# The loop over further expert blocks moved between the 24th and the 25th expert, the last block's results in float32, sums of squares as products with ones

## The chip, the cores and the metric

One core of a Trainium2 chip runs the whole program. The metric is the device time of one execution in microseconds (us); the median of the runs counts. Five engines work side by side, each through its own list of instructions: PE multiplies matrices, DVE and ACT work on vectors, POOL on vectors and scattered transfers, and SP issues the transfers of the weights. They wait for each other, and for transfers, by semaphores.

## The reference

Two layers. Each is a mixer (state space, attention, long convolution; the change only touches what it receives) and then a mixture of 32 experts, of which every token uses two. At the end comes a normalisation.

```python
def _rms_norm(x, g):
    xf = x.astype(jnp.float32)
    y = xf * lax.rsqrt(jnp.mean(xf * xf, axis=-1, keepdims=True) + EPS)
    return (y * g.astype(jnp.float32)).astype(x.dtype)

def _hier_moe(h, w_group, w_expert, w1, w3, w2):
    ...
    g_w, g_idx = lax.top_k(g_prob, 1)
    top_v, top_i = lax.top_k(in_group, MOE_TOP_K)
    gate = jax.nn.softmax(top_v, axis=-1) * g_w
    ...
    def expert_block(args):
        xb, e = args
        return (jax.nn.silu(xb @ w1[e]) * (xb @ w3[e])) @ w2[e]
    ...
    ys = ys.reshape(n_rows, d) * row_w[:, None].astype(h.dtype)
    return jnp.zeros_like(h).at[row_tok].add(ys)

def reference(x, c, ctx, ...):
    for i in range(DEPTH):
        hl = _modulate(xl, norm1_g[i], mod_l[0], mod_l[1])
        ...
        xl = xl + mod_l[5] * y          # y: the experts' sum for each token
    return _rms_norm(xl, final_g)
```

Width 1024, 256 latent tokens and 256 context tokens; the experts' hidden width is 512. Layer 0 treats all 512 tokens, layer 1 the 256 latent ones.

## The kernel before, in words

The residual stream xT lies transposed in the chip's memory: 128 partitions times 8 pieces (k) of the width, with the tokens as columns (512 in layer 0, 256 in layer 1).

Each expert has one block of 64 places for tokens. Its weights are 12 pages of 512 KB: 8 pages w13 (w1 beside w3) and 4 pages w2. SP issues their loads in the order of use, through 8 semaphores that it takes in turn, so each load waits for the one 8 before it: 8 loads are in flight. `Stream.pump` holds how many pages SP may be ahead of PE: 18 in layer 0 from the 17th expert on, 30 in layer 1. All pages come from one pool of 44.

For each expert PE runs `first_half` (w13: 16 products, L1582), waits for ACT and DVE (`swiglu`, then `turn`), and runs `second_half` (w2: 8 products, L1606). Then `scaled_result` takes the 64x1024 results times the token's weight as a rounded high part and the remainder: ACT, DVE, ACT, DVE, one after the other (L118, L1718). Two experts share a tile of 128 rows; `combine` brings the pair before back to its tokens by two products per k with a 0/1 matrix GT (L1688), and `residual` adds them to xT on DVE (L1620). Those products fill the gaps of the next experts.

Layer 0 always runs a 33rd block for the first expert with more than 64 tokens. Whatever is still left over goes through a loop whose count is read from the data (`tc.For_i`, L1900). With this data the count is 0 in both layers: no row of the trace comes from the loop's body. The loop stands at the end of each layer's experts.

`combine_last` brings the last block back (layer 1: the last pair), spreads k over more banks of PSUM and interleaves squares of xT (ACT) and their sum (DVE); for k = 0, 2, 4 the addition runs on ACT and POOL. After the loop the sum of squares goes through `rstd_columns` (products with ones into columns of 1, square root, reciprocal of 128x4 or 128x2) and is spread back over rows by transposes (L217). Layer 0 hands this to the first projections of layer 1; layer 1 to the final stage (L1956, then the output's transfers).

Experts are counted from 0 here: e = 24 is the 25th.

Of the kernel before, what the change touches and what calls it, by code (L numbers as in the profile page):

```python
# [69 lines left out]
def build(tc, A, dbg=None):  # L70
# [1333 lines left out]
    def moe(i, pctx, router, ws, last_part):  # L1404
# [380 lines left out]
        def extra_result(b, inf1):  # L1785

            Y_[-1] = [page(F32R) for _ in range(2)]
            scaled_result(Y_[-1], b, inf1[:, 1:2], slice(0, CAP))
            GT_[-1] = wk([128, n], "GT", 2, F32R)
            nc.vector.tensor_scalar(GT_[-1][0:CAP], iotaN[0:CAP, 0:n], inf1[0:CAP, 0:1], None, op0=OP.is_equal)  # L1790
# [286 lines left out]
```

## Time and profile before

| | us |
|---|---|
| runs | 1707.82, 1708.36, 1708.34 |
| median | 1708.34 |
| profiled execution, its own time | 1709.9 |
| its span | 1708.1 |
| PE busy | 1533.8 |
| DVE busy | 888.6 |
| ACT busy | 482.4 |

The span is the time from the first to the last instruction; 1.8 us of the execution's own time lie around it. PE is busy for 90% of the span, but that is a mean over stages, so the places that the change touches are read by themselves: e = 24 of layer 0 begins at 796.12 us, the hand-off of layer 0 at 944.29 us (the end of the 33rd block's w2 products), e = 24 and e = 31 of layer 1 begin at 1564.07 and 1671.08 us, and layer 1's w2 products end at 1686.56 us.

### The profile page before, as it was taken

What the parts mean: (1) busy time and instruction counts of PE and PEld (TensorE: products, weight loads), DVE (VectorE), ACT (ScalarE), POOL (GpSimd) and SP (SyncE); (2) the same over time, 40 slices, a digit from 0 to 9 for tenths busy, and PEclk for the clock granted to TensorE, in tenths of its full rate; (3) what the DMA queues carried; (4) which work ended last, traced back from release to release, by engine and by line L of the source; (5) the groups of instructions that cost most, each with busy time, mean ns of one, the idle gap of its engine ahead of it and who ended that gap; (6) DMA issues with size and microseconds to landing.
All of it is one profiled execution on the core that took longest, in us unless ns stands there. A gap on an engine that the chain in (4) does not pass through costs nothing. (4 is left out here: it accounts for less than half of the span.)

```text
span 1708.1 us, 22533 instructions
## 1 busy us (share of the span) xinstructions
PE 1533.8 (90%) x8073; PEld 788.0 (46%) x8073; DVE 888.6 (52%) x2176; ACT 482.4 (28%) x931; POOL 94.7 (6%) x154
## 2 busy tenths in 40 slices
PE   5888889998999999999899597899799999999995
PEld 1676744476433333344233387547534444333322
DVE  6769565545244546864643758455524434333333
ACT  3343544342111121112122534444311111111112
POOL 0000212003000000002000000010100000000000
PEclk9998899998999999999999698998899999999998
DMA  9111244559999999999999112577799999999994
GB/s 343 64 38 62 79 181 162 218 198 351 374 392 407 409 409 409 409 408 372 373 402 409 61 62 99 205 264 267 293 359 409 409 409 409 409 409 409 409 409 184
DMA packets 143300, 510.04 MB, mean 299 GB/s; under 512 B 17995, under 2 KB 18573, under 8 KB 142929
## 3 DMA queue, kind: packets, MB, share of 16 engines
q1 hardware_dynamic: 138736, 495.21, 75.0%
q0 software_dynamic: 4160, 12.82, 2.2%
q8 instruction: 66, 1.08, 0.3%
q10 hardware_dynamic: 288, 0.52, 0.1%
q14 instruction: 50, 0.40, 0.1%
HBM read 504.85 MB, written 3.64 MB: 298 GB/s over the span
## 5 line engine op out<-in xcount | busy, mean ns | idle before, releaser
L1582 PE MATMUL MOEp<-MOEpg,MOEpg 128*64 128x512 f32 x956 | 227.4, 603 | 13.1 <-DMA MOEpg<-in_w 11.9
L1582 PE MATMUL MOEp<-MOEpg,ROUTpg 128*64 128x512 f32 x960 | 220.5, 603 | 8.2 <-DMA MOEpg<-in_w 7.9
L1718 DVE SCALAR_TENSOR_TENSOR MOEpg<-MOEpY,MOEwt,MOEpg 64x512 fp32r<-64x512 f32 x128 | 96.0, 750 | 241.5 <-ACT MOEpg L118 241.4
L1606 PE MATMUL MOEpY<-MOEpg,MOEhT 128*64 128x512 f32 x960 | 219.4, 599 | 1.8 <-DVE MOEhT L1598 1.8
L1620 DVE SCALAR_TENSOR_TENSOR zxT<-MOEpC,zmod,zxT 128x256 f32<-128x256 f32 x385 | 168.2, 479 | 8.2 <-PE MOEpC L1698 2.1
L118 ACT ACTIVATE MOEpg<-MOEpY,MOEwt 64x512 fp32r<-64x512 f32 x128 | 87.3, 682 | 276.3 <-PE MOEpY L1606 212.2
L1588 DVE TENSOR_TENSOR MOEh<-MOEh,MOEp 128x256 f32<-128x256 f32 x65 | 27.3, 420 | 241.9 <-ACT MOEh L118 241.9
L118 ACT ACTIVATE MOEh<-MOEp 128x256 f32<-128x256 f32 x65 | 24.9, 383 | 399.7 <-PE MOEp L1582 399.7
L1688 PE MATMUL MOEpC<-MOEGT,MOEpg 128*128 128x512 f32 (+1 forms) x496 | 130.0, 364 | 6.7 <-DVE zxT L1620 6.0
L1582 PEld LDWEIGHTS MOEp<-MOEpg,ROUTpg 128*64 128x64 f32 x960 | 64.2, 137 | 149.4 <-issue 103.7
L1582 PEld LDWEIGHTS MOEp<-MOEpg,MOEpg 128*64 128x64 f32 x956 | 59.4, 136 | 159.3 <-DMA MOEpg<-in_w 90.5
L1606 PEld LDWEIGHTS MOEpY<-MOEpg,MOEhT 128*64 128x64 f32 x960 | 63.5, 136 | 120.6 <-issue 93.8
L1688 PEld LDWEIGHTS MOEpC<-MOEGT,MOEpg 128*128 128x128 f32 x496 | 75.2, 189 | 61.7 <-issue 26.8
L166 PE MATMUL ADAb<-ADApg,zcact 128*32 128x512 f32 x384 | 76.1, 614 | 12.8 <-DMA ADApg<-in_adaw 12.8
L788 PE MATMUL PROJb<-INPpg,PROJpg 128*128 128x512 f32 (+1 forms) x384 | 73.8, 356 | 6.4 <-DVE PROJpg L974 5.7
L788 PEld LDWEIGHTS PROJb<-INPpg,PROJpg 128*128 128x128 f32 x384 | 63.5, 206 | 15.9 <-ACT PROJpg L118 6.7
L118 ACT ACT_TABLE_LOAD x35 | 44.9, 1283 | 15.7 <-DVE ATTst L1102 5.7
L1657 PE MATMUL MOEpG<-MOEpg,ROUTpg 128*128 128x256 f32 x240 | 44.7, 310 | 1.1 <-DVE MOEpg L1493 1.1
L1657 PEld LDWEIGHTS MOEpG<-MOEpg,ROUTpg 128*128 128x128 f32 x240 | 33.0, 194 | 24.2 <-issue 15.8
L1091 PE MATMUL ATTb<-QKVpg,QKVpg 96*128 96x512 f32 x64 | 35.4, 654 | 7.3 <-ACT ATTpg L118 7.3
L1373 PE MATMUL OUTb<-OUTpg,ATTpg 128*128 128x512 f32 (+1 forms) x192 | 41.3, 380 | 0.0
L1373 PEld LDWEIGHTS OUTb<-OUTpg,ATTpg 128*128 128x128 f32 x192 | 34.9, 214 | 5.3 <-DVE ATTpg L230 0.2
(541 smaller groups left out, 2115.2 us busy)
## 6 DMA issues: line engine op xcount, KB each, us to landing
MOEpg<-in_w SPq DMA_DIRECT2D x719, 512.0 KB
ADApg<-in_adaw SPq DMA_DIRECT2D x96, 512.0 KB
ROUTpg<-in_w SPq DMA_DIRECT2D x61, 512.0 KB
PROJpg<-in_win SPq DMA_DIRECT2D x16, 512.0 KB
ATTpg<-in_wout SPq DMA_DIRECT2D x8, 512.0 KB
OUTpg<-in_wout SPq DMA_DIRECT2D x8, 512.0 KB
QKVpg<-in_uq SPq DMA_DIRECT2D x5, 512.0 KB
MOEpg<-in_win SPq DMA_DIRECT2D x5, 512.0 KB
```

What stands on the lines that cost most here:

```text
L118: nc.scalar.activation(out, in_, f, **kw)
L166: nc.tensor.matmul(b[q:q + 32, :], cact[:, k, :], w[:, h * 512:(h + 1) * 512], start=(k < 2), stop=(k >= KD - 2), tile_position=(0, q))
L788: nc.tensor.matmul(b, a_[:, c], b_[k][:, c0:], start=(first and n == 0), stop=(last and n == 2))
L1091: nc.tensor.matmul(b, qc[h][:, nq - NS + qt * 128:nq - NS + (qt + 1) * 128], kc[h], start=True, stop=True)
L1373: nc.tensor.matmul(b, a_[:, c], y_, start=(n == 0 and j == 0), stop=(n == KD - 1 and j == 2))
L1582: nc.tensor.matmul(b[64 * h:64 * h + 64, :], X[:, k, :], w[:, h * 512:(h + 1) * 512], start=(k == 0), stop=(k == KD - 1), tile_position=(0 ...
L1588: nc.vector.tensor_mul(h_, h_, b[:, 256:512])
L1606: nc.tensor.matmul(b[64 * h:64 * h + 64, :], hT[:, k % 2, (k // 2) * 64:(k // 2) * 64 + 64], w[:, h * 512:(h + 1) * 512], start=(k == 0), ...
L1620: nc.vector.scalar_tensor_tensor(xT[:, k, seg(s)], b[:, s * NS - c0:(s + 1) * NS - c0], mod[:, 40 + k, s:s + 1], xT[:, k, seg(s)], op0=OP. ...
L1657: nc.tensor.matmul(b[:, kk * 256:(kk + 1) * 256], hs[t][:, k * 128:(k + 1) * 128], G[:, t].rearrange("p e c -> p (e c)"), start=(t == 0 an ...
L1688: nc.tensor.matmul(b, Y_[p][j][rows, k * 128:(k + 1) * 128], GT_[p][rows], start=(j == 0), stop=(j == 1))
L1718: nc.vector.scalar_tensor_tensor(Y[1][rows_of, h * 512:(h + 1) * 512], b[rows], wt[rows], yh.bitcast(F32), op0=OP.mult, op1=OP.subtract)
```

## The change

```diff
+FURTHER = 24
+    def rstd_rows(b, r, nch):
+        act(r, b, AF.Sqrt, scale=1.0 / nch, bias=epsT)
+        nc.vector.reciprocal(r, r)
+        return r
...
-            rstd1 = rstd_of(None, D, acc=acc)
-            first_projections(rstd1)
+            first_projections(acc)
...
+        def combine_last(y, gt):
+            total = pb("pT")[:, 0:n]
+            for k in range(KD + 3):
+                if k < KD:
+                    b = pb(*tags[k % 5])[:, 0:n]
+                    nc.tensor.matmul(b, y[:, k * 128:(k + 1) * 128], gt, start=True, stop=True)
+                    if i == 0 and k in (0, 3):
...
+                    else:
+                        residual(b, k)
+                if 1 < k < KD + 2:
+                    sq[k - 2] = squares()[:, 0:n]
+                    act(sq[k - 2], xT[:, k - 2, c0:], AF.Square)
+                if k > 2:
+                    nc.tensor.matmul(total, ones2[:, 0:1].to_broadcast([128, 128]), sq.pop(k - 3),
+                                     start=(k == 3), stop=(k == KD + 2))
+            return rstd_rows(total, squares()[:, 0:n], D)
...
+        def places(idx, wt, rows):
+            nc.vector.tensor_scalar(gt, iotaN[rows, 0:n], idx, wt, op0=OP.is_equal, op1=OP.mult)
+        def plain_result(b, rows):
+            y = page()[rows]
+            for h in range(2):
+                copy(h, y[:, h * 512:(h + 1) * 512], b[64 * h:64 * h + 64])
...
+        def last_hook(k):
+            last = NE // 2 - 1
+            if k < 4:
+                combine(last - 1, [4 + k])
+            else:
+                combine(last, [2 * k - 8, 2 * k - 7], slice(0, CAP))
...
-            for e in range(NE):
+            for e in range(FURTHER):
+                expert(e)
+        further_blocks()
+        with tc.manual_schedule():
+            for e in range(FURTHER, NE):
+                expert(e)
...
-        nc.vector.memset(item, 0.0 if i == 0 else -1.0)
-        with tc.For_i(0, nc.values_load(items, min_val=0, max_val=2 * NT // CAP), 1):
```

In words: (1) the loop stands between e = 23 and e = 24 in both layers; its body, which does not run, uses 2 pages as a ring and adds straight into xT. (2) The last block (layer 0: the 33rd; layer 1: e = 31) keeps its results plain, half copied by ACT and half by DVE; the token's weight is in GT; one float32 product per k takes the place of two. In layer 1, e = 30 is brought back inside `first_half` of e = 31, by `last_hook`, with the four products left of the pair before. (3) The squares are summed by float32 products with ones in all 128 rows, so the sum stands in every partition; square root and reciprocal then run over 128x512 (layer 0) or 128x256 (layer 1), and `rstd_columns` and the transposes go. (4) POOL adds for k = 0 and 3 in layer 0 only; the final gain is loaded early.

The next pieces are the programs' orders, one row per instruction, with what it waits for; DMAHW0 to 7 are the eight semaphores of SP's loads, DMASW those of POOL's, and the "_49" says nothing here. First SP, before, at the loop of layer 1: the branches follow the last loads of expert weights (the last page of e = 31).

```order
L114 DMA MOEpg_12371<-in_w 128x1024 [waits DMAHW5_49,PE_49]
L114 DMA MOEpg_12375<-in_w 128x1024 [waits DMAHW6_49,PE_49]
L114 DMA MOEpg_12379<-in_w 128x1024 [waits DMAHW7_49,PE_49]
L114 DMA MOEpg_12383<-in_w 128x1024 [waits DMAHW0_49,PE_49]
L114 DMA MOEpg_12387<-in_w 128x1024 [waits DMAHW1_49,PE_49]
L114 DMA MOEpg_12391<-in_w 128x1024 [waits DMAHW2_49,PE_49]
L1900 COMPARE_AND_BRANCH
L1900 UNCONDITIONAL_BRANCH [waits SP_sequencer_49,DMAHW0_49,DMAHW1_49,DMAHW2_49,DMAHW3_49,DMAHW4_49,DMAHW5_49,DMAHW6_49,DMAHW7_49]
```

SP now, at the same loop: the row ahead of the branch is the load of page 317 (counted from 1), that is of the 5th page of e = 26.

```order
L115 DMA MOEpg_11758<-in_w 128x1024 [waits DMAHW4_49,PE_49]
L115 DMA MOEpg_11792<-in_w 128x1024 [waits DMAHW5_49,PE_49]
L115 DMA MOEpg_11796<-in_w 128x1024 [waits DMAHW6_49,PE_49]
L115 DMA MOEpg_11800<-in_w 128x1024 [waits DMAHW7_49,PE_49]
L115 DMA MOEpg_11804<-in_w 128x1024 [waits DMAHW0_49]
L1915 COMPARE_AND_BRANCH
L1915 UNCONDITIONAL_BRANCH [waits SP_sequencer_49,DMAHW0_49,DMAHW1_49,DMAHW2_49,DMAHW3_49,DMAHW4_49,DMAHW5_49,DMAHW6_49,DMAHW7_49]
L1915 UNCONDITIONAL_BRANCH [waits DMASW3_49,DMASW4_49,DMASW2_49,DMASW5_49,DMASW1_49,DMAHW0_49,SP_sequencer_49,DMAHW1_49,DVE_sequencer_49,DMAHW2_49,PE_sequencer_49,DMAHW3_49,Activation_sequencer_49,DMAHW4_49,Pool_sequencer_49,DMAHW5_49,D
```

The loop, with the waits for all eight semaphores, moved from behind page 384 to behind page 317 of layer 1 (in layer 0 from behind the last page to behind page 305).

PE, before, in `first_half` of an expert of layer 1 (of the two names behind the arrow, the first is the page of weights).

```order
L1582 MATMUL MOEp_2527_11773<-MOEpg_11567,MOEpg_11094 64x512 [waits DMAHW3_49]
L1582 MATMUL MOEp_2527_11773<-MOEpg_11567,MOEpg_11094 64x512
L1582 MATMUL MOEp_2527_11773<-MOEpg_11585,MOEpg_11094 64x512 [waits DMAHW4_49]
L1582 MATMUL MOEp_2527_11773<-MOEpg_11585,MOEpg_11094 64x512
L1582 MATMUL MOEp_2527_11773<-MOEpg_11590,MOEpg_11094 64x512 [waits DMAHW5_49]
L1582 MATMUL MOEp_2527_11773<-MOEpg_11590,MOEpg_11094 64x512
L1582 MATMUL MOEp_2527_11773<-MOEpg_11594,MOEpg_11094 64x512 [waits DMAHW6_49]
L1582 MATMUL MOEp_2527_11773<-MOEpg_11594,MOEpg_11094 64x512
```

PE now, behind the loop: the last branch of the loop and the beginning of e = 24's `first_half`.

```order
L1915 COMPARE_AND_BRANCH
L1915 UNCONDITIONAL_BRANCH [waits DMASW5_49,DMASW4_49,DMASW6_49,DMASW3_49,DMASW7_49,DMASW2_49,DMAHW0_49,DMASW1_49,DMAHW1_49,DMASW0_49,DMAHW2_49,SP_sequencer_49,DMAHW3_49,DVE_sequencer_49,DMAHW4_49,PE_sequencer_49,DMAHW5_49,Activation_s
L1588 MATMUL MOEp_2582_12022<-MOEpg_11572,MOEpg_11450 64x512 x2
L1588 MATMUL MOEp_2582_12022<-MOEpg_11606,MOEpg_11450 64x512 x2
L1588 MATMUL MOEp_2582_12022<-MOEpg_11610,MOEpg_11450 64x512 x2
L1588 MATMUL MOEp_2582_12022<-MOEpg_11614,MOEpg_11450 64x512 x2
L1588 MATMUL MOEp_2582_12022<-MOEpg_11618,MOEpg_11450 64x512 x2
```

The waits of the products for their single pages are gone there: behind the loop's branches the pages issued ahead of it are taken as landed.

PE, before, at the end of layer 1: the pair's products for k = 6 and 7 of the pair before, then the last pair's, two a k.

```order
L1688 MATMUL MOEpC_12539<-MOEGT_12434,MOEpg_12353 128x256
L1688 MATMUL MOEpC_12543<-MOEGT_12434,MOEpg_12352 128x256 [waits DVE_49]
L1688 MATMUL MOEpC_12543<-MOEGT_12434,MOEpg_12353 128x256
L1698 MATMUL MOEpC_12549<-MOEGT_12547,MOEpg_12478 128x256 [waits DVE_49,Activation_49]
L1698 MATMUL MOEpC_12549<-MOEGT_12547,MOEpg_12479 128x256
L1698 MATMUL MOEpC_12555<-MOEGT_12547,MOEpg_12478 128x256
L1698 MATMUL MOEpC_12555<-MOEGT_12547,MOEpg_12479 128x256
L1698 MATMUL MOEpG_12559<-MOEGT_12547,MOEpg_12478 128x256
L1698 MATMUL MOEpG_12559<-MOEGT_12547,MOEpg_12479 128x256
L1698 MATMUL MOEpY_12566<-MOEGT_12547,MOEpg_12478 128x256
L1698 MATMUL MOEpY_12566<-MOEGT_12547,MOEpg_12479 128x256
L1698 MATMUL MOEp_2723_12571<-MOEGT_12547,MOEpg_12478 128x256 [waits Activation_49]
```

PE now, in `first_half` of e = 31, between two pages of w13 (L1694 is `combine`, L1588 the w13 products).

```order
L1694 MATMUL MOEpC_12672<-MOEGT_12621,MOEpg_12607 128x256 [waits DVE_49]
L1694 MATMUL MOEpC_12672<-MOEGT_12621,MOEpg_12608 128x256
L1588 MATMUL MOEp_2732_12623<-MOEpg_12500,MOEpg_12021 64x512 [waits DMAHW2_49]
L1588 MATMUL MOEp_2732_12623<-MOEpg_12500,MOEpg_12021 64x512
L1694 MATMUL MOEpC_12678<-MOEGT_12621,MOEpg_12607 128x256 [waits DVE_49]
L1694 MATMUL MOEpC_12678<-MOEGT_12621,MOEpg_12608 128x256
```

PE now, behind e = 31's `second_half`: L1711 are the products that bring it back, one a k, and L1724 those with ones.

```order
L1711 MATMUL MOEpC_12712<-MOEGT_12686,MOEpg_12708 128x256 [waits Activation_49]
L1711 MATMUL MOEpC_12715<-MOEGT_12686,MOEpg_12708 128x256
L1711 MATMUL MOEpG_12718<-MOEGT_12686,MOEpg_12708 128x256
L1711 MATMUL MOEpY_12723<-MOEGT_12686,MOEpg_12708 128x256 [waits DVE_49]
L1724 MATMUL MOEpT_12711<-MOEpg_12721,zones_14_82 128x256 [waits PE_49,Activation_49]
L1711 MATMUL MOEp_2757_12728<-MOEGT_12686,MOEpg_12708 128x256
L1724 MATMUL MOEpT_12711<-MOEpg_12721,zones_14_82 128x256 [waits Activation_49]
L1711 MATMUL MOEpC_12734<-MOEGT_12686,MOEpg_12708 128x256 [waits DVE_49]
L1724 MATMUL MOEpT_12711<-MOEpg_12731,zones_14_82 128x256 [waits Activation_49]
L1711 MATMUL MOEpC_12739<-MOEGT_12686,MOEpg_12708 128x256 [waits DVE_49]
```

The pair before and e = 30 moved into the w13 half; what is left behind w2 is one product a k and one a sum of squares.

## Rows read from the trace of the kernel before

**Rows 1.** The page's section 2: what the transfers moved, in 40 equal slices.

```profile
GB/s 343 64 38 62 79 181 162 218 198 351 374 392 407 409 409 409 409 408 372 373 402 409 61 62 99 205 264 267 293 359 409 409 409 409 409 409 409 409 409 184
```

**Rows 2.** Windows: length, busy us by engine, granted clock, DMA share, GB/s.

```profile
1336.00:1390.00 54.00, 53.87 (x270) 22.62 (x272) 21.84 (x58) 9.11 (x20) 0.00 (x0) 1.00 1.03 409
...
1626.00:1671.00 45.00, 39.97 (x174) 12.10 (x170) 13.83 (x40) 5.03 (x9) 0.00 (x0) 1.00 1.03 409
```

**Rows 3.** Timeline of PE in layer 1: start, us, instruction, count, [idle before].

```profile
1335.88 7.09 PE L1582 MATMUL MOEp<-MOEpg,MOEpg 128*64 128x512 f32 x32
...
1348.58 0.74 PE L1688 MATMUL MOEpC<-MOEGT,MOEpg 128*128 128x256 f32 x4
1349.25 1.51 PE L1582 MATMUL MOEp<-MOEpg,MOEpg 128*64 128x512 f32 x6
...
1564.07 4.79 PE L1582 MATMUL MOEp<-MOEpg,MOEpg 128*64 128x512 f32 x20
...
1679.20 1.08 PE L1582 MATMUL MOEp<-MOEpg,MOEpg 128*64 128x512 f32 x4 [0.20 <-DMA MOEpg<-in_w]
```

**Rows 4.** Timeline of SP, layer 0 (to 945) and layer 1 (to 1690): start, us, count.

```profile
796.15 133.70 SPq L114 DMA_DIRECT2D MOEpg<-in_w  x93
...
1563.96 110.48 SPq L114 DMA_DIRECT2D MOEpg<-in_w  x87
```

**Rows 5.** DMA issues, 1500 to 1600 us, then 790 to 830: KB, us to landing.

```profile
MOEpg<-in_w SPq DMA_DIRECT2D x79, 512.0 KB
...
S5cpg<-kscr POOLq DMA_DIRECT2D x16, 64.0 KB, 8.4
```

**Rows 6.** Timeline around the loop of layer 1 (no instruction of its body ran).

```profile
1697.58 0.42 DVE L1709 TENSOR_TENSOR MOEpg<-MOEpg,MOEpg 128x256 f32<-128x256 f32 x1
...
1698.96 1.01 PE L201 MATMUL FINb<-zones,MOEpg 128*128 128x2 f32 x4 [4.54 <-DVEq L1900]
```

**Rows 7.** Timeline of PE from 615: a pause and the w13 half behind it.

```profile
615.84 2.03 PE L570 MATMUL SPECpX<-SPECpg,SPECpg 128*128 128x512 f32 x2 [1.52 <-DVE MOEpg L576]
617.81 7.82 PE L1582 MATMUL MOEp<-MOEpg,ROUTpg 128*64 128x512 f32 x32
```

**Rows 8.** Timeline of layer 1's end: w2, its first results, the output's scaling.

```profile
1682.91 3.65 PE L1606 MATMUL MOEpY<-MOEpg,MOEhT 128*64 128x512 f32 x16 [1.01 <-DVE MOEhT L1598]
...
1686.61 0.68 ACT L118 ACTIVATE MOEpg<-MOEpY,MOEwt 64x512 fp32r<-64x512 f32 x1 [4.29 <-PE MOEpY L1606]
1687.33 0.74 DVE L1718 SCALAR_TENSOR_TENSOR MOEpg<-MOEpY,MOEwt,MOEpg 64x512 fp32r<-64x512 f32 x1 [4.02 <-ACT MOEpg L118]
...
1701.26 3.22 DVE L1956 SCALAR_TENSOR_TENSOR fo<-zxT,fg,FINb 128x256 f32<-128x256 f32 x8 [0.78 <-PE FINb L217]
```

**Rows 9.** Lines by form: four float32 products (two records each), busy us, mean ns.

```profile
L921 PE MATMUL S5db<-S5dpg,S5dpg 128*128 128x512 f32 x8 | 3.6, 592 | 0.0
...
L921 PE MATMUL S5db<-S5dpg,S5dpg 128*128 128x256 f32 x8 | 1.9, 379 | 0.0
```

**Rows 10.** Lines by form: DVE's reciprocals, busy us, mean ns.

```profile
L1109 DVE RECIPROCAL ATTst<-ATTst 128x4 f32<-128x4 f32 x8 | 1.4, 176 | 7.7 <-ACT ATTpg L118 7.7
...
L376 DVE RECIPROCAL S5apg<-S5apg 128x16 f32<-128x16 f32 x1 | 0.3, 253 | 0.0
```

**Rows 11.** Lines of PE, 810 to 936 us: w13 products, busy, idle before.

```profile
L1582 PE MATMUL MOEp<-MOEpg,ROUTpg 128*64 128x512 f32 x224 | 56.8, 622 | 8.2 <-DMA MOEpg<-in_w 7.9
...
L1582 PE MATMUL MOEp<-MOEpg,MOEpg 128*64 128x512 f32 x32 | 7.5, 602 | 0.2 <-DMA MOEpg<-in_w 0.2
```

**Rows 12.** Timeline of layer 0's end: last w2, two subtractions, first scaled piece.

```profile
940.64 3.65 PE L1606 MATMUL MOEpY<-MOEpg,MOEhT 128*64 128x512 f32 x16
...
967.19 2.36 DVE L230 TENSOR_TENSOR S5bpg<-MOEpg,S5bpg 128x1024 fp32r<-128x1024 f32 x2 [0.77 <-ACT S5bpg L118]
...
969.46 1.65 DVE L224 SCALAR_TENSOR_TENSOR INPpg<-zxT,zA,MOEb 128x256 f32<-128x256 f32 x4
```

**Rows 13.** Windows: layer 0's hand-off, then the end of layer 1.

```profile
961.00:971.00 10.00, 3.05 (x13) 2.56 (x13) 6.35 (x9) 7.75 (x10) 0.00 (x0) 0.50 0.20 52
...
1691.00:1695.00 4.00, 3.43 (x16) 3.13 (x16) 2.41 (x6) 2.92 (x8) 2.20 (x3) 0.57 0.00 0
```

More of the change, by code (lines that the diff above doesn't have):

```diff
@@ L1783, in extra_turn @@
             return X
[L1785 to L1790, printed above, removed]
+        def places(idx, wt, rows):
+            gt = wk([128, n], "GT", 2, F32R).bitcast(F32)[rows]
+            nc.vector.tensor_scalar(gt, iotaN[rows, 0:n], idx, wt, op0=OP.is_equal, op1=OP.mult)
+            return gt
+        def plain_result(b, rows):
+            y = page()[rows]
+            for h in range(2):
+                copy(h, y[:, h * 512:(h + 1) * 512], b[64 * h:64 * h + 64])
+            return y
         squares = halves()
@@ new lines, in further_blocks, with refilled @@
+        def further_blocks():
+            nc.vector.memset(item, 0.0 if i == 0 else -1.0)
+            with tc.For_i(0, nc.values_load(items, min_val=0, max_val=2 * NT // CAP), 1):
+                nc.vector.tensor_scalar(item, item, 1.0, None, op0=OP.add)
+                ereg, G1, ax = extra_choose(item)
+                ring = [page() for _ in range(2)]
+                def refilled():
+                    for k, src in enumerate(extra_weights(ereg)):
+                        nc.sync.dma_start(ring[k % 2], src)
+                        yield ring[k % 2]
+                w = refilled()
+                xt, inf1 = extra_gather(G1, ax)
+                X1 = extra_turn(xt)
+                h_ = wk([128, 256], "h", 1)
+                hT = wk([128, 2, 128], "hT", 1)
+                swiglu(first_half(X1, w), h_)
+                turn(h_, hT)
+                gt = places(inf1[0:CAP, 0:1], inf1[0:CAP, 1:2], slice(0, CAP))
+                y = plain_result(second_half(hT, w), slice(0, CAP))
+                combine_plain(y, gt, range(KD))
@@ L1883, in moe @@
             if i == 0:
-                b = first_half(X1, pages)
+                inf1 = final["info"]
+                final["gt"] = places(inf1[0:CAP, 0:1], inf1[0:CAP, 1:2], slice(0, CAP))
+                b = first_half(final["X"], pages)
                 h_ = wk([128, 256], "h", 1)
@@ L1947, in build @@
             routing_constants()
+        else:
+            fin = ctx.enter_context(tc.tile_pool(name="fin", bufs=1))
+            fg = fin.tile([128, KD], F32, name="fg", tag="fg")
+            nc.sync.dma_start(fg, A["fg"])
         acc = moe(i, *m)
     stage[0] = "FIN"
[L1950 to L1959 removed]
+    o4 = [page().rearrange("p (k c) -> p k c", k=4) for _ in range(2)]
+    for k in range(KD):
+        nc.vector.scalar_tensor_tensor(o4[k // 4][:, k % 4], xT[:, k, NS:], fg[:, k:k + 1], acc, op0=OP.mult, op1=OP.mult)
+        if k in FIN:
+            f = k + 1 - FIN[k]
+            (nc.sync if k % 4 == 1 else nc.scalar).dma_start(A["out"][:, f:k + 1], o4[k // 4][:, f % 4:k % 4 + 1])
     ctx.close()
```

186 lines of the change are left out of this document (81 added, 105 removed).

## The prediction

> **What bounds the kernel now.** I read the 40 slices first: through the last quarter the transfers move 409 GB/s without a gap [rows 1]. The windows then tell who waits. In the middle of layer 1 PE is busy 53.87 of 54 us: it is the bound, and SP runs up to its limit of 30 pages ahead. Late in layer 1, at the same 409 GB/s, PE is busy only 39.97 of 45 us: the lead is used up and the transfers are the bound [rows 2]. At 409 GB/s a page of 524,288 bytes takes 1.28 us, which agrees with 79 loads in 100 us [rows 5]. PE's timeline gives the same by expert: PE-bound, one expert takes 13.37 us (1335.88 to 1349.25), where its twelve pages take 15.4. From e = 24 (1564.07) to the end of e = 31's w13 half, whose last page comes late (1679.20 and 1.08), it is 116.2 us, where PE alone would need seven times 13.37 and one half of 7.09, in all 100.7 [rows 3]. So PE has 15.5 us of slack there, and no more; this is the number against which the moved loop is weighed.
>
> **The moved loop, layer 1.** Here the orders decide. At the loop SP waits for all eight load semaphores, and behind it PE's w13 products carry no wait for their pages any more. That can only be sound if nothing passes the loop, skipped or not, before every load issued ahead of it has landed. The order has 317 of the 384 pages ahead of it (288 used by e = 23 and 29 ahead). So the lead, which keeps PE fed, has to land while PE stands.
>
> When e = 24 begins, how much of that lead is missing? The row of SP from 1563.96 holds the last 87 loads [rows 4]: 297 were issued, and 317 is the 20th of the row. Its issue is 19 x 1.28 later, at 1588.3. Eight loads are in flight, so it lands 8 x 1.28 = 10.2 us later, at 1598.5. The loop's own branches cost 0.96 us in the trace (DVE ends at 1698.00, PE starts at 1698.96) [rows 6]. PE resumes at 1599.5 instead of 1564.07: +35.4.
>
> Of that the slack gives back 15.5: behind the loop 29 pages lie ready, and the other 67 take 67 x 1.28 = 86 us plus a start of a few us, while PE works 101 us, so PE is the bound to the end. Left: +19.9. It is less only if load 317 lands earlier than the row of SP says: with fewer than eight really under way it would be 1 to 5 less. A slow start of the queue behind the loop changes nothing as long as the lead lasts.
>
> A pause also lowers PE's clock. The row for that: behind pauses of 1.5 and 2.2 us, a w13 half took 7.82 instead of 7.09 us [rows 3, 7]. One such start per loop: +0.7 (bounds 0 and 3, four times as long for a pause that is far longer).
>
> **e = 31 in layer 1.** Twelve `combine` calls stand in its w13 half now. Before, the experts were waiting for transfers there; now PE is the bound, so they cost their full time: two calls take 0.67 us (1348.58 to 1349.25) [rows 3], so 12 x 0.33 = +4.0. (Four of them left other places where they partly filled gaps; I count that as nothing, bound -1.) The first of them come straight behind e = 30's w2 products and ahead of e = 31's first page; the third needs a bank of PSUM that DVE frees only behind e = 30's `scaled_result`, four passes in a row of 0.68, 0.74, 0.68 and 0.76 (the first two stand in [rows 8]). PE's queue behind it is the whole w13 half. I take +2.8; the bounds are 0, if DVE gets to the bank first, and 2.9, the whole of the four passes.
>
> **Layer 1's tail.** Before, from the end of w2 (1682.91 + 3.65 = 1686.56) to the end of the last scaling (1701.26 + 3.22 = 1704.48) it is 17.9 us [rows 8]. Now: two plain copies side by side, 0.74 by the longer row plus 0.1 of hand-over = 0.85; 8 products that bring the block back and 8 with ones, float32: eight records of 128x256 took 1.9 us, four products [rows 9], at the pipelined spacing 0.43 each, so 16 x 0.43 = 6.9, and DVE keeps up with one pass of some 0.4 a k; hand-overs 0.3; square root of 128x256 0.42 (an estimate from ACT's 0.68 for 512 columns); reciprocal of 128x256; scaling 3.2 [rows 8]. The trace has no such reciprocal. From 176 ns for 4 columns to 253 ns for 16 it grows by 6.4 ns a column [rows 10], so 256 columns take about 1.75 and 512 about 3.3. The lower bound is the scaling's pace, 0.40 per 128x256 (eight in 3.22) [rows 8]; an upper one, if the first columns hide the real pace, twice the value, 3.5. Sum 13.4: -4.5. The loop's branches and the columns' products and transposes are in that difference.
>
> The Trainium skill, "VectorE: DVE Perf Modes", section "First, the fixed hardware budget", says that a reciprocal is an iterative divide with a repeat count of 8, and its "Specifications" give 0.96 GHz; an estimate from that page is 2.1 us for 256 columns and 4.3 for 512. The rows show 6.4 ns a column, not 8.3. By the page the sum would be 1.4 us higher.
>
> **Layer 0.** The order has 305 pages ahead of the loop (288 and 17). The row of SP from 796.15 holds the last 93 of 396 loads [rows 4]: 303 were issued, so 305 is issued at 797.4 and lands at about 807.7; with 0.96 for the branches PE resumes at 808.6 to 809.4. (Two of POOL's 16 gathers, 8.4 us to landing [rows 5], stand ahead of the loop too, and are in by then.) PE loses 13 us and 0.7 for the clock. But from 810 on PE waits for pages for longer than that: the 256 w13 records take 64.3 us busy and 8.4 idle [rows 11], where eight halves at 7.09 [rows 3] are 56.7. That is 16.0 of slack, so the transfers stay the bound. What counts is their own pause, from 807.7 until the first load behind the loop moves bytes, 2 to 4 us; POOL's other 14 gathers, which take from the weights' bandwidth anyway, fill part of it. I take +1.5; bounds 0 (all filled) and 4.
>
> The hand-off: from the end of w2 (944.29) 0.85 for the copies; the first bank comes free about 0.9 later, at 946.0; then 16 float32 products of 128x512, 0.86 each at full clock (3.6 us for four, as above) [rows 9], 13.8, to 959.8; square root 0.7, reciprocal 3.3, and on DVE four subtractions ahead of the first scaled piece, two of them 2.36 in the trace, 4.7; that makes 968.5 to 968.9 against 969.46 [rows 12]: -0.5. Bounds: -3 (the reciprocal at the scaling's pace) and +13 (the products at the low clock).
>
> **Sum.** Layer 1: 19.9 + 0.7 + 4.0 + 2.8 - 4.5 = 22.9. Layer 0: 1.5 - 0.5 = 1.0. Together +23.9. The profiled execution took 1709.9 us, 1.6 over the median of the runs, so 1733.8 on its scale is 1732.2 as a median.
>
> **The rivals.**
> Tail only: the skipped loop doesn't wait for transfers in flight, or its wait is over before PE gets there. Then the lead stays, the 0.96 us hide under the transfers, the 12 calls in e = 31 cost some 2 us (its w13 half waits that long for pages), and the tail's -4.5 and the hand-off's -0.5 remain: about -3, 1705. It decides from the point where the loop's exit lets PE go before load 317. For it: the trace of before can't show the opposite, since at its loops no page is under way. Against: PE's rows behind the loop have no waits.
>
> Transfers stay the bound in layer 1 too: only their pause of some 3 us counts, and the tail gives it back, 1708 to 1710. It would take a lead that is mostly landed at 1564; against it stands the row of SP, 20 pages short.
>
> Low clock in the tails: the granted clock was 0.57 in layer 1's last products and 0.50 in the hand-off [rows 13], 1.2 GHz or between. Then the tail's 16 products cost 6.9 more and layer 0's up to 13.8: 1740 to 1753. For it: these windows, and the pause of PE for the copies. Against: PE was idle half of that time, whereas now its float32 products stand back to back.
>
> **How the numbers follow.** Forecast 0.78; low clock in the tails, in one of them at least, 0.13; tail only 0.05; transfers the bound 0.04. Below, the forecast's own range takes its bounds: 1 for the calls, 2.8 for the bank, 1.5 for layer 0's pause, 2.5 for the hand-off, 1 for layer 1's reciprocal, 5 for an earlier landing, in all 13.8; they are not met at once, and eight tenths of them give 1721. Above, 2.3 for the clock, 2.5 for layer 0's pause, 1.75 and 3.3 for reciprocals at twice the value, in all 9.9; six tenths give 1738. The low clock in one tail reaches to 1744, so 1721 to 1744. Faster by over 0.2% (3.4 us, about what a measurement of this kernel can tell from no change) needs the tail-only case or better, 0.04; within 0.2% 0.03; slower 0.93.
>
> **What would show it.** In the profile after: PE idle from about 1564 to 1599 in layer 1 and from 796 to 809 in layer 0, released by the loop's line; a hole in the slices of GB/s behind each; w13 halves at 7.09 us without waits for pages from there to the end of layer 1; a reciprocal of about 1.75 and one of 3.3 us; 16 products at 0.43 us behind the last w2. I am wrong if PE's pause in layer 1 is under 15 us, if PE waits for pages again late in layer 1, or if the reciprocals cost ten times what the rows say.

## The result, and the profile after

The changed kernel takes 1776.0 us (median of four runs, 1765.03 to 1777.81) against 1708.35: slower by a ratio of 1.0381 (95% interval 1.0338 to 1.0423, estimated over all runs). The forecast was 1732.2, in a range of 1721 to 1744. The sign was right; of the 65 us more in the profiled execution (1775.61, span 1773.7) it accounted for 24.

I set both profiles side by side at six marks and give what each stretch between two marks grew by. The marks are the starts and ends of PE's products: the end of the 33rd block's w2, the first projection product of layer 1, the first w13 product of layer 1, the end of e = 30's w2, the end of e = 31's w2, and on DVE the end of the last scaling.

| stretch | before, us | after, us | grew by | forecast |
|---|---|---|---|---|
| layer 0, to the end of the 33rd block's w2 | 944.29 | 949.99 | +5.7 | +1.5 |
| hand-off | 26.64 | 39.58 | +12.9 | -0.5 |
| mixer of layer 1 | 252.46 | 271.27 | +18.8 | 0 |
| layer 1, e = 0 to e = 30 | 447.09 | 470.54 | +23.4 | +22.7 |
| e = 31, to the end of its w2 | 16.08 | 23.31 | +7.2 | +4.7 |
| tail | 17.92 | 15.21 | -2.7 | -4.5 |
| sum | | | +65.3 | +23.9 |

The last column splits the forecast's terms at the same marks. Its loop term, 19.9 + 0.7, sets 15.5 us of slack against the pause, up to the end of e = 31's w13 half. Of these, 2.1 stand in e = 31 itself (its half took 9.2 us before, from 1671.08 to 1680.28, where PE alone needs 7.09), so the loop's +20.6 is +22.7 up to e = 30, and the +6.8 of e = 31 is +4.7.

So the moved loop cost in layer 1 about what was forecast; two stretches that I had at next to nothing, the mixer and the hand-off, make 32 of the 41 us that were missed.

The 40 slices of the page after, to be read against [rows 1]: the GB/s have three holes that were not there or not so deep, one in layer 0 (283, where before had 372), one in layer 1's mixer (the 120 between 194 and 355), one at layer 1's loop (356).

```profile
GB/s 338 54 42 54 149 133 238 196 190 387 356 408 408 409 409 409 409 409 283 409 401 172 48 84 149 194 120 355 268 410 409 409 409 409 409 409 356 408 369 24
```

PE's timeline after, at the two loops; in brackets the idle time ahead and what ended it (L1915 is the loop's line, on SP):

```profile
810.86 1.97 PE L1588 MATMUL MOEp<-MOEpg,ROUTpg 128*64 128x512 f32 x4 [14.63 <-SPq L1915]
...
1600.53 0.72 PE L1694 MATMUL MOEpC<-MOEGT,MOEpg 128*128 128x256 f32 x4
1636.80 3.54 PE L1588 MATMUL MOEp<-MOEpg,MOEpg 128*64 128x512 f32 x8 [35.55 <-SPq L1915]
```

The pause in layer 1 is as forecast (35.4); that in layer 0 is 14.6 us, where I had 13. What PE waits for from layer 1's loop to the end (view of waits of PE, 1600 to 1760: total us, times, longest): no page of weights any more, so PE is the bound there, as forecast.

```profile
PE MOEp L1588 <- SPq L1915: 35.5, 1, 35.5
PE MOEpC L1694 <- DVE zxT L1626: 3.0, 1, 3.0
PE MOEpT L1603 <- DVE MOEh L1594: 2.4, 4, 0.9
```

In e = 31 PE's timeline also shows four records of w13 at two lengths; the granted clock is 0.58 from 1735 to 1739 and 0.99 from 1739 to 1743.

```profile
1735.47 1.85 PE L1588 MATMUL MOEp<-MOEpg,MOEpg 128*64 128x512 f32 x4
...
1739.93 1.08 PE L1588 MATMUL MOEp<-MOEpg,MOEpg 128*64 128x512 f32 x4
```

Now the stretch that was not in the forecast at all. SP's timeline after, in layer 1's mixer:

```profile
1139.25 0.33 SPq L667 DMA_DIRECT2D ROUTpg<-in_router  x1
1182.18 0.33 SPq L1999 DMA_DIRECT2D fg<-in_fg  x1
1182.60 1.33 SPq L115 DMA_DIRECT2D ATTpg<-in_wout  x3
1184.02 5.82 SPq L115 DMA_DIRECT2D ADApg<-in_adaw  x8
1191.39 19.68 SPq L115 DMA_DIRECT2D ROUTpg<-in_w  x16
1212.05 5.43 SPq L115 DMA_DIRECT2D OUTpg<-in_wout  x5
```

and the view of waits of SP from 1139 to 1185:

```profile
SPq L1999 <- DVE ATTpg L1118: 42.5, 1, 42.5
```

Between 1139.6 and 1182.2 SP issues nothing. It stands in front of a load of 4 KB, the final gain (fg), which the change moved ahead of layer 1's experts; by its waits, the tile it is written to takes memory that the mixer's attention on DVE gives back only at 1182. Before, the same queue issued the first output weights, the first expert weights and the last five output weights in these rows:

```profile
1131.84 4.49 SPq L114 DMA_DIRECT2D ATTpg<-in_wout  x3
...
1145.23 24.18 SPq L114 DMA_DIRECT2D ROUTpg<-in_w  x16
1170.38 16.50 SPq L114 DMA_DIRECT2D OUTpg<-in_wout  x5
```

After, these go at 1182.60, 1191.39 and 1212.05. Who waits is in PE's view of waits (1100 to 1262), in a row that before did not have; ACT's timeline leads from there back to the load, which was issued at 1212.05 and took 10.2 us to land:

```profile
PE OUTb L1379 <- ACT OUTpg L119: 15.1, 1, 15.1
...
1222.23 1.06 ACT L119 ACTIVATE OUTpg<-OUTpg 128x1024 fp32r<-128x1024 f32 x1 [28.72 <-DMA OUTpg<-in_wout]
```

The hand-off: in the profile after, the granted clock is 0.50, the 1.2 GHz level, while PE is busy without a gap. Windows after (length, busy us of PE and others, clock, DMA share, GB/s):

```profile
944.00:948.00 4.00, 3.65 (x15) 1.42 (x16) 3.22 (x8) 0.37 (x1) 0.00 (x0) 1.00 1.03 410
...
952.00:956.00 4.00, 3.60 (x6) 1.52 (x7) 1.91 (x5) 1.10 (x3) 1.26 (x1) 0.75 0.00 0
...
960.00:968.00 8.00, 8.00 (x9) 1.98 (x9) 1.75 (x4) 1.89 (x3) 0.21 (x1) 0.50 0.00 0
```

A product of 128x512 takes 2.0 us there (two records, 961.93 to 963.93), where 0.86 was forecast. In the tail of layer 1 the clock stayed at 1.00. Timelines after of both reciprocals:

```profile
980.35 3.35 DVE L224 RECIPROCAL MOEpg<-MOEpg 128x512 f32<-128x512 f32 x1 [5.41 <-ACT MOEpg L119]
...
1764.85 1.75 DVE L224 RECIPROCAL MOEpg<-MOEpg 128x256 f32<-128x256 f32 x1 [1.94 <-ACT MOEpg L119]
```

3.35 and 1.75 against 3.3 and 1.75 worked out from [rows 10] at 6.4 ns a column; from 256 to 512 columns it is 6.2.

### The profile page after: what moved, and what is told of

It is laid out like the page before. It is cut to its first block, busy times and chain, and to the rows that moved or that the text cites. A ratio compares the mean times of both kernels' runs of the same rounds, so it can differ in the third digit from the quotient of the medians.

```text
span 1773.7 us, 22573 instructions
## 1 busy us (share of the span) xinstructions
PE 1553.0 (88%) x8103; PEld 800.9 (45%) x8103; DVE 890.2 (50%) x2174; ACT 476.2 (27%) x921; POOL 91.1 (5%) x150
## 5 line engine op out<-in xcount | busy, mean ns | idle before, releaser
L1588 PE MATMUL MOEp<-MOEpg,MOEpg 128*64 128x512 f32 x956 | 222.9, 606 | 40.9 <-SPq L1915 35.5
L1588 PE MATMUL MOEp<-MOEpg,ROUTpg 128*64 128x512 f32 x960 | 215.0, 601 | 14.6 <-SPq L1915 14.6
L1626 DVE SCALAR_TENSOR_TENSOR zxT<-MOEpC,zmod,zxT 128x256 f32<-128x256 f32 x394 | 172.3, 479 | 23.9 <-PE MOEpC L1711 9.4
L1694 PE MATMUL MOEpC<-MOEGT,MOEpg 128*128 128x512 f32 (+2 forms) x512 | 134.0, 363 | 9.5 <-DVE zxT L1626 8.9
L1588 PEld LDWEIGHTS MOEp<-MOEpg,MOEpg 128*64 128x64 f32 x956 | 63.1, 137 | 172.7 <-issue 125.0
L1588 PEld LDWEIGHTS MOEp<-MOEpg,ROUTpg 128*64 128x64 f32 x960 | 66.9, 138 | 148.4 <-issue 131.9
L1694 PEld LDWEIGHTS MOEpC<-MOEGT,MOEpg 128*128 128x128 f32 (+1 forms) x512 | 77.9, 190 | 69.8 <-issue 30.7
L1379 PE MATMUL OUTb<-OUTpg,OUTpg 128*128 128x256 f32 (+1 forms) x192 | 34.6, 337 | 15.1 <-ACT OUTpg L119 15.1
L1663 PEld LDWEIGHTS MOEpG<-MOEpg,ROUTpg 128*128 128x128 f32 x240 | 32.8, 194 | 26.7 <-issue 14.6
## 6 DMA issues: line engine op xcount, KB each, us to landing
MOEpg<-in_w SPq DMA_DIRECT2D x719, 512.0 KB, 10.2
OUTpg<-in_wout SPq DMA_DIRECT2D x8, 512.0 KB, 10.2
```

The costliest lines, as they stand in the source:

```text
L1379: nc.tensor.matmul(b, a_[:, c], y_, start=(n == 0 and j == 0), stop=(n == KD - 1 and j == 2))
L1588: nc.tensor.matmul(b[64 * h:64 * h + 64, :], X[:, k, :], w[:, h * 512:(h + 1) * 512], start=(k == 0), stop=(k == KD - 1), tile_position=(0 ...
L1626: nc.vector.scalar_tensor_tensor(xT[:, k, seg(s)], b[:, s * NS - c0:(s + 1) * NS - c0], mod[:, 40 + k, s:s + 1], xT[:, k, seg(s)], op0=OP. ...
L1663: nc.tensor.matmul(b[:, kk * 256:(kk + 1) * 256], hs[t][:, k * 128:(k + 1) * 128], G[:, t].rearrange("p e c -> p (e c)"), start=(t == 0 an ...
```

## The experiments

All are compared with runs of the kernel before on the same chip. Where a run is set against the marks above, that is from its profiled execution.

**e1_fg_late: the gain's load behind the last pages.**

```diff
-            nc.sync.dma_start(fg, A["fg"])
+            late.append(lambda: nc.sync.dma_start(fg, A["fg"]))
...
             last = NE // 2 - 1
+            for f in late:
+                f()
```

> The changed kernel, with one thing undone: the load of the final gain is issued behind the last expert's pages instead of in the mixer of layer 1. Theory A: that load waits 42 us (1140 to 1182) for DVE and ACT to give back the memory it is written to, and all of SP's weight loads wait behind it; PE then waits 15 us for the last output products. Undone, the time falls by 17 to 20 us, to about 1757 (1746 if the hand-off of layer 0 runs at full clock). Rival B: the 15 us come from the hand-off's late start; then the time stays near 1776.

Measured: 1750.36 us, ratio 1.0247 (1.0203 to 1.0290). The mixer of layer 1 takes 249.9 us, 21 less than after, and SP issues the first output weights at 1138.07. Theory A stands. The runs lie at two levels: 1743.69 and 1743.81, 1756.90 and 1757.42. The profile is of a run of the lower one, and its hand-off takes 28.5 us instead of 39.6, at clock 1.00:

```profile
950.30:970.00 19.70, 16.93 (x36) 5.82 (x36) 7.97 (x18) 8.05 (x15) 2.52 (x2) 1.00 0.01 3
```

With the 39.6 of the profile after, the hand-off costs 2 or 13 us more than before's, by the clock that is granted. The two upper runs of e1 have a lower mean clock over their span (0.938 and 0.940 against 0.949 and 0.951), but no profile; that it fell in their hand-off is likely and not shown. The fourth run of the changed kernel, 11 us below the other three, has a higher one (0.944 against 0.935) and no profile either; a hand-off at the full clock would fit it.

**e2_before_fg_early: the same load, put early in the kernel before.**

```diff
             routing_constants()
+        else:
+            fin0 = ctx.enter_context(tc.tile_pool(name="fin0", bufs=1))
+            fg = fin0.tile([128, KD], F32, name="fg", tag="fg")
+            nc.sync.dma_start(fg, A["fg"])
...
-        fg = fin.tile([128, KD], F32, name="fg", tag="fg")
-        nc.sync.dma_start(fg, A["fg"])
```

> The kernel before, with this one part of the change: the final gain is loaded ahead of layer 1's experts. Theory A: 17 to 20 us more, 1725 to 1728. Rival B: no difference, 1708.

Measured: 1730.18 us, ratio 1.0119 (1.0101 to 1.0138), 20 us more and 2 above the expectation. SP issues nothing from 1123.0 to 1162.8, where the load stands. The mixer takes 268.5 us (252.5 before); PE's row of the output products shows the same wait as after:

```profile
1204.31 0.80 PE L1373 MATMUL OUTb<-OUTpg,OUTpg 128*128 128x256 f32 x2 [15.27 <-ACT OUTpg L118]
```

One load of 4 KB alone costs 20 us here. With e1 it is shown from both sides.

**e3_loop_last: the loop just ahead of combine_last.**

```diff
-            for e in range(FURTHER):
-                expert(e)
-        further_blocks()
-        stage[0] = "MOE"
-        with tc.manual_schedule():
-            for e in range(FURTHER, NE):
+            for e in range(NE):
                 expert(e)
...
+        further_blocks()
+        stage[0] = "MOE"
+        with tc.manual_schedule():
             acc = combine_last(final["y"], final["gt"])
```

> As e1_fg_late, and the loop stands at the end of the experts, just ahead of combine_last, in both layers; the rest of the change stays. Theory A (the loop waits for the lead to land): layer 1 gets back some 25 us and layer 0 some 6; what is left is the hand-off (+13 at the low clock, 0 at the full one) and the tail (-2): 1708 to 1722. Rival C (the loop costs little, the float32 products and the reciprocals cost the rest): 1745 to 1755.

Measured: 1738.67 us, ratio 1.0154 (1.0128 to 1.0181), between the two expectations. The stretch from e = 0 to e = 30 of layer 1 falls to 448.1 us (447.1 before): the middle loop's price is gone, as A says. But three other prices show: the hand-off at the low clock, 42.4 us; e = 31, 25.7 (16.1 before); and the tail 24.0, since the loop's branches now stand between w2 and the products that bring it back. Behind them the granted clock falls there too, to 0.50 from 1722 to 1734, and a product of the tail takes 1.15 us instead of 0.63, which is the larger part of the 9 us that the tail is longer than after's 15.2. PE's and ACT's rows there, with the idle time that the loop ends:

```profile
1718.11 1.28 ACT L119 ACT_TABLE_LOAD   x1 [1.34 <-DVEq L1915]
1718.27 1.71 PE L1711 MATMUL MOEpC<-MOEGT,MOEpg 64*128 64x256 f32 x4 [2.12 <-DVEq L1915]
...
1724.03 0.48 DVE L1626 SCALAR_TENSOR_TENSOR zxT<-MOEp,zmod,zxT 128x256 f32<-128x256 f32 x1 [1.82 <-PE MOEp L1711]
```

**e4_lead: few pages ahead of the loop.**

```diff
-            while len(self.pages) < min(len(self.src), self.used + self.limit):
+            while len(self.pages) < min(len(self.src), self.used + self.limit, self.cap):
...
             for e in range(FURTHER):
+                if e == 20:
+                    ws.cap = FURTHER * (KD + 4) + (8 if i == 0 else 9)
                 expert(e)
+        ws.cap = 1000
         further_blocks()
```

> As e1_fg_late, with the loop in its new place between e = 23 and e = 24, but SP may issue only 8 (layer 0) and 9 (layer 1) pages beyond e = 23 ahead of the loop, about what it has issued anyway when PE gets there; behind the loop the old limits hold. Theory A: PE's pause in layer 1 falls from 36 to about 11 us and the transfers stay the bound to the end, so layer 1 pays 4 to 6 us for the loop instead of some 28 and layer 0 about 3 instead of 6: 1728 to 1735 with the hand-off at the low clock, 1717 to 1724 at the full one. Rival C (the pause is the price of the branches or of loading code, not of the landing): no change against e1_fg_late, about 1757.

Measured: 1730.65 us, ratio 1.0107 (1.0083 to 1.0131). The median lies inside A's expectation for the low clock, but that is partly luck: the profiled run, which has the low clock (hand-off 39.6), took 1740.38, above the expectation, and the other three, 1725.08 to 1731.68, have a higher clock over their span. The profile's rows are the better test. PE's row at layer 1's loop:

```profile
1594.26 3.68 PE L1588 MATMUL MOEp<-MOEpg,MOEpg 128*64 128x512 f32 x8 [9.82 <-SPq L1915]
```

The pause is 9.8 us instead of 35.5 with 20 pages less ahead of the loop; e = 0 to e = 30 takes 452.4 us, +5.3 instead of +23.4. The branches are the same: what PE waits for is the landing.

**e6_early: layer 1's loop between e = 7 and e = 8.**

```diff
-FURTHER = 24
+FURTHER = (24, 8)
...
-            for e in range(FURTHER):
+            for e in range(FURTHER[i]):
```

> As e1_fg_late, but the loop of layer 1 stands between e = 7 and e = 8. Theory A: the wait there is as before for 29 pages of lead, of which some 5 are not issued: PE stands 16 to 18 us; but from there to the end PE has over 25 us of slack, so all of it is given back and only the pause of the transfers (3 to 4 us) stays: from layer 1's first w13 product to the end of e = 30's w2 about 451 us instead of 471. Rival C (the price is in the branches or the code): 471 as in e1_fg_late.

Measured: 1733.79 us, ratio 1.0131 (1.0100 to 1.0162). PE's row at the loop:

```profile
1370.33 9.39 PE L1588 MATMUL MOEp<-MOEpg,MOEpg 128*64 128x512 f32 x32 [16.07 <-SPq L1915]
```

A pause of 16.1 us, and yet e = 0 to e = 30 takes only 452.9 us, 5.8 more than before: PE waits for pages again late in the layer (from 1593 us on), so about two thirds of the pause are given back. The expectation was 451. Together with e4 this shows both halves of the forecast's sum, the landing and the slack.

**e5_k128: products of 128 rows for the last block.**

```diff
+            if padded:
+                nc.gpsimd.memset(gt[CAP:] if rows.start == 0 else gt[0:CAP], 0.0)
...
-            y = page()[rows]
+            y = page()
+            if padded:
+                nc.gpsimd.memset(y[CAP:] if rows.start == 0 else y[0:CAP], 0.0)
```

> As e1_fg_late, but the products that bring the last block back have 128 rows instead of 64 (the other 64 rows of both operands are zero). In the changed kernel's tail a product of 64 rows behind one of 128 starts its weight load only when the one before has ended: 0.63 us a product instead of 0.43. Theory D (the change of rows costs 0.2 us each time): the tail of layer 1 falls from 15.2 to 12.5 to 13 us, and the hand-off by some 2.5 at the full clock. Rival E (each float32 product of 128x256 takes 0.63 in this mix, by its operands or its semaphores): tail stays 15.2.

Measured: 1741.05 us, ratio 1.0181 (1.0159 to 1.0202). The tail falls to 13.5 us. PE's timeline there, after and then in e5_k128 (PEld is the load of the weights):

```profile
1756.34 0.59 PE L1711 MATMUL MOEpG<-MOEGT,MOEpg 64*128 64x256 f32 x2
1756.77 0.59 PE L1711 MATMUL MOEpY<-MOEGT,MOEpg 64*128 64x256 f32 x2
1757.29 0.70 PE L1724 MATMUL MOEpT<-MOEpg,zones 128*128 128x256 f32 x2
1757.92 0.29 PEld L1711 LDWEIGHTS MOEp<-MOEGT,MOEpg 64*128 64x128 f32 x2 [0.33 <-issue]
1757.92 0.70 PE L1711 MATMUL MOEp<-MOEGT,MOEpg 64*128 64x256 f32 x2
...
1758.55 0.70 PE L1724 MATMUL MOEpT<-MOEpg,zones 128*128 128x256 f32 x2
1759.18 0.70 PE L1711 MATMUL MOEpC<-MOEGT,MOEpg 64*128 64x256 f32 x2
1759.80 0.70 PE L1724 MATMUL MOEpT<-MOEpg,zones 128*128 128x256 f32 x2
```

```profile
1725.70 0.41 PEld L1711 LDWEIGHTS MOEp<-MOEGT,MOEpg 128*128 128x128 f32 x2
1725.91 0.59 PE L1711 MATMUL MOEp<-MOEGT,MOEpg 128*128 128x256 f32 x2
1726.35 0.59 PE L1724 MATMUL MOEpT<-MOEpg,zones 128*128 128x256 f32 x2
1726.78 0.59 PE L1711 MATMUL MOEpC<-MOEGT,MOEpg 128*128 128x256 f32 x2
1727.21 0.60 PE L1724 MATMUL MOEpT<-MOEpg,zones 128*128 128x256 f32 x2
```

In e5 the products follow each other at 0.43 us, as forecast from [rows 9]; after, at 0.63 wherever the rows change, and at 0.43 between two products of 64 rows (1756.34 and 1756.77). In e5 the weights' load begins 0.21 us ahead of its product, while the product before still runs; after, it begins together with its product. Theory D stands: it is the change between 64 and 128 rows that costs 0.2 us. The gain, 1.7 us, is smaller than the 2.2 to 2.7 expected.

The second effect was not expected: the four runs lie within 1.7 us (1740.45 to 1742.11), and the hand-off of the profile takes 27.0 us at clock 1.00. Of seven profiles with float32 products of 64 rows (after, e1, e3, e4, e6, e7, e8) five have the low clock in the hand-off, of two with 128 rows (e5, e10) none. Two of the seven (e1, e8) stay at the full clock as well, so two profiles are too few to show that the rows are the cause.

**e7_hook: the twelve calls from the 5th page on.**

```diff
-            if k < 4:
-                combine(last - 1, [4 + k])
-            else:
-                combine(last, [2 * k - 8, 2 * k - 7], slice(0, CAP))
+            for c in {4: (-4, -3), 5: (-2, -1, 0), 6: (1, 2, 3), 7: (4, 5, 6, 7)}.get(k, ()):
+                combine(*((last - 1, [8 + c]) if c < 0 else (last, [c], slice(0, CAP))))
```

> As e1_fg_late, but the twelve combine calls in e = 31's w13 half start ahead of its 5th page instead of its 1st. Theory F (PE waits for a bank of PSUM behind e = 30's scaled_result, and the pause lowers the clock): from the end of e = 30's w2 to the end of e = 31's w13 half 11.7 to 12.5 us instead of 17.8. Rival G (the twelve calls themselves cost it, by DVE's additions): 16 to 18 us.

Measured: 1750.64 us, ratio 1.0229 (1.0195 to 1.0262), the same as e1. The stretch is 13.9 us, between both expectations: the wait for the bank is gone (PE goes from one half to the next without a gap), but the calls cost 6.3 us and not 4.0, at a clock of 1.00. PE now waits for DVE's additions between them:

```profile
1720.14 0.47 PE L1694 MATMUL MOEpC<-MOEGT,MOEpg 64*128 64x256 f32 x2 [0.44 <-DVE zxT L1626]
...
1725.15 0.89 PE L1694 MATMUL MOEpC<-MOEGT,MOEpg 64*128 64x256 f32 x4 [0.34 <-DVE zxT L1626]
...
1729.19 6.37 PE L1612 MATMUL MOEpY<-MOEpg,MOEhT 128*64 128x512 f32 x16 [0.52 <-DVE MOEhT L1604]
```

The last row took back the rest: w2 ran at the 1.2 GHz level, 6.37 us instead of 3.65.

**e8_bridge: products in the hand-off's gap.**

```diff
                 combine(last, range(6, KD))
+                b = pb("p13", 1 + i)
+                for _ in range(3):
+                    nc.tensor.matmul(b, ident, iotaN, start=True, stop=True)
```

> As e1_fg_late, with three float32 products of 128x512 whose result nothing reads, placed in layer 0's hand-off ahead of combine_last, where PE idles 1.3 us. Runs of e1_fg_late lie at two levels 13 us apart, 1743.7 and 1757, and the profile of the first has the hand-off at the full clock (28.5 us), that of the changed kernel at the half (39.6). Theory H (the idle gap decides whether the clock falls): all runs at the upper level of clock, 1743 to 1746. Rival I (the clock falls by the mix of products, whatever the gap): two levels as in e1_fg_late, or all low, 1757 and above.

Measured: 1748.28 us, ratio 1.0231 (1.0202 to 1.0259). The profile's hand-off is at the full clock, 29.8 us, but the runs lie at two levels again (1745.12 and 1745.26, 1751.31 and 1751.65), nearer to each other than in e1. Neither theory is met as stated: the upper runs have a lower clock over their span (0.943 and 0.945 against 0.948 and 0.949), but no profile that shows where it fell. What lets the clock fall is not settled by this.

**e9_pair_plain: what is left of the change, in the kernel before.** Only layer 1's end: e = 30 and e = 31 plain in one page, products of 128 rows, sums with ones, the gain's load behind the last pages; the loop behind the sums, as before.

```diff
+                    for h in range(2):
+                        copy(h, final["y"][half, h * 512:(h + 1) * 512], b[64 * h:64 * h + 64])
...
-            acc = combine_last(-1, slice(0, CAP)) if i == 0 else combine_last(last)
+            acc = combine_last(-1, slice(0, CAP)) if i == 0 else combine_pair(final["y"], final["gt"])
```

> The kernel before with what the experiments left of the change for layer 1's end alone: e = 30 and e = 31 are both kept plain in one page, 64 rows each, and one float32 product of 128 rows a k brings both back with their weights in GT (no calls in e = 31's w13 half, no 64-row products); the squares are summed by products with ones; square root and reciprocal over 128x256; the loop stays where it was, behind the sums, and its body would sum anew; the gain's load stands behind the last pages. Layer 0 is that of before. Theory: the 16 products as in e5_k128, the tail there 13.5, plus 2 us for the loop's branches and the table load that they bring: from the end of w2 to the end of the last scaling 15 to 16 us instead of 17.9, so 1 to 3 us faster than before. Rival: behind the loop's pause the clock is low and ACT loads its table late, 18 to 20 us, no gain or slower.

Measured in 12 runs against 17: 1709.62 and 1710.64 us, ratio 0.9997 (0.9986 to 1.0008): the same. The tail is 17.0 us instead of 17.9. ACT's and DVE's rows tell why it is not 15:

```profile
1694.72 0.42 ACT L118 ACTIVATE MOEpg<-zxT 128x256 f32<-128x256 f32 x1 [0.45 <-DVE zxT L1626]
1696.86 1.28 ACT L118 ACT_TABLE_LOAD   x1 [1.72 <-PEq L1942]
1698.16 0.47 ACT L118 ACTIVATE FINpg<-MOEp,zeps 128x256 f32<-128x256 f32 x1
1698.66 1.75 DVE L223 RECIPROCAL FINpg<-FINpg 128x256 f32<-128x256 f32 x1 [3.98 <-ACT FINpg L118]
```

The loop's branches and the table load put 2.3 us between the last product (ended 1695.9) and the square root, and the wide reciprocal costs 1.75 where the narrow one costs 0.17.

**e10_k128_lead: e4 and e5 together.**

> As e1_fg_late, with both e4_lead (few pages ahead of the loop) and e5_k128 (128 rows). If the prices add, it is before + 3 (loop, layer 0) + 5 (loop, layer 1) + 8 (the calls in e = 31) - 4 (tail) + 0 (hand-off at the full clock): 1719 to 1723, every run within 3 us. Rival I (the clock in the hand-off falls whatever the rows): some of the four runs 10 us and more above the others.

Measured: 1728.20 us, ratio 1.0105 (1.0089 to 1.0122), 5 us over the expected range. Hand-off 27.0 at clock 1.00, tail 13.5, as in e5; e = 0 to e = 30 452.2 us, as in e4. Layer 0 gives nothing back here (+6.4 at its end; e4 had +3.1), and e = 31 costs +8.2. The runs lie within 4.3 us, more than the 3 expected and less than the 10 that rival I asked for.

## Why the prediction was wrong

- **The moved loop, layer 1: right.** The lead (the pages issued ahead of PE) has to land, 35.4 us forecast, 35.5 measured; the slack behind it is given back. Up to e = 30 the stretch grew by 23.4 instead of 22.7; the start behind the pause took 1.6 us more in e = 24's w13 half (8.69 us instead of 7.09), where I had 0.7. e4 changed the landing and e6 the slack behind it, and both terms followed.
- **The step that failed first: the load of the final gain.** The part on the change names no price for it at all; I read the early load as a row that goes out of the tail. A moved load counts on the queue that it is moved past: it waits 42.5 us for memory at the head of SP's queue, and the loads of output weights and expert weights stand behind it. +18.8 in the profile, +20 alone (e2), -21 when undone (e1). SP's timeline after has that load between two loads of the mixer, behind the wait for DVE; of SP's order I had shown and read only the stretches at the loops.
- **The step that failed second: "16 float32 products of 128x512, 0.86 each at full clock".** The row that this rests on is a stretch at the full clock [rows 9], while the rows of the very place showed 0.50 [rows 13]. I held the low clock to be one rival of 0.13, and argued against it that the products now stand back to back; from 960 to 968 they did, and the clock was 0.50. In five of seven profiles it came in the hand-off, and in the changed kernel not in the tail: 2.0 us a product, +12.9 instead of -0.5, near the upper bound of +13 that I had worked out and then given little weight. The range ended at 1744, though that rival's own price for the hand-off, 13.8, reaches 1746. In e1, at the full clock, the hand-off is 28.5 where the forecast has 26.1; of these 2.4 us, 1.5 are the change of rows (27.0 in e5, without it).
- **Layer 0's loop: wrong in the bound.** The pause is 14.6 us instead of 13, and +5.7 instead of +1.5 is left. "so the transfers stay the bound" is the step that failed: from 810 to 945 PE waits for no page any more. The pause, 1.6 for the start behind it (8.65 instead of 7.09), 2.8 for DVE and 2.2 for a w2 half make 21.2 us, against 16.0 of slack. The last two are in e = 25: its `swiglu` waits for DVE, which sets up the 33rd block, and the w2 half behind that ran at the low clock. Before, DVE's same work (816.9 to 821.8) stood beside PE's waits for pages, and the low clock behind them cost 1.6 us; all of that I had taken as slack. First the timeline of before, then that of after:

```profile
819.46 1.08 PE L1582 MATMUL MOEp<-MOEpg,ROUTpg 128*64 128x512 f32 x4 [2.33 <-DMA MOEpg<-in_w]
820.91 3.53 PE L1582 MATMUL MOEp<-MOEpg,ROUTpg 128*64 128x512 f32 x8 [0.38 <-DMA MOEpg<-in_w]
```

```profile
838.38 0.69 PE L1603 MATMUL MOEpT<-zident,MOEh 128*128 128x128 f32 x2 [2.83 <-DVE MOEh L1594]
...
840.38 5.82 PE L1612 MATMUL MOEpY<-MOEpg,MOEhT 128*64 128x512 f32 x16
```

- **e = 31: short by 2.5** (+7.2 for +4.7). The wait for the bank is right (3.0 for 2.8). The calls cost 5.4 us and not 4.0, and behind the wait the low clock takes 1.6 more, which I had at nothing; the gap ahead of w2 shrank by 0.7. That +7.2 is close to the +6.8 that I had added up is luck: 2.1 us of the waits for pages went away in the same stretch. In e7 DVE's additions are part of the calls' price.
- **Tail: the sign right, the size short** (-2.7 for -4.5). The products' pace, 0.63 instead of 0.43, is the term; e5 gave the forecast pace back and 1.7 us with it.
- **The rivals.** Tail only and transfers as the bound are refuted by the pause of 35.5 us and by e3, e4 and e6. Of the two tails the low clock came in the hand-off alone.
- **The reciprocals: right**, 3.35 and 1.75 us. The estimate of 4.3 and 2.1 us that I had drawn from the Trainium skill, "VectorE: DVE Perf Modes", "First, the fixed hardware budget" and "Specifications" (a repeat count of 8, at 0.96 GHz), is too high here; the measurement decides.

What stays open: what lets PE's clock fall in the hand-off. Rows show only that it fell within a few us of the last w2 half in five of seven profiles with products of 64 rows, and in none of two without. The idle time ahead of the first product does not decide it: 1.28 us after, where the clock falls, and 1.28 in e1 and 1.27 in e5, where it stays.

## What to carry to other kernels

Loads in flight are part of a loop's price, even of one that is skipped: here it waited until all that was issued had landed (35.5 us with 29 pages of lead, 9.8 with 9), so it belongs where little is under way, or where the stage has slack behind it. A load that is moved earlier is not free because it is small: look what its tile waits for and what is queued behind it. A duration for a new operation is to be taken from rows at the clock that its place has, not from the nearest row of the same shape.

## What the runs showed of the hardware

- Between a float32 product of 128 rows and one of 64 rows, the second one's weight load does not begin while the first still runs as it does between products of equal rows: 0.63 us a product of 128x256 instead of 0.43 (after), gone when zeros pad it to 128 rows (e5).
- PE can stay at the 1.2 GHz level while it is busy without a gap: 8.00 of 8.00 us at 0.50, from 960 to 968 (after).
- DVE's float32 reciprocal grows by 6.2 to 6.4 ns a column: 0.253 us for 128x16, 1.75 for 128x256, 3.35 for 128x512.
- A loop that is skipped holds PE until the loads issued ahead of it have landed: 35.5 us with 29 pages of 512 KB ahead (after), 9.8 with 9 (e4).
- A load of 4 KB that waits for its memory holds all that SP issues behind it: 42.5 us after, and 20 us of the kernel's time alone (e2).
